# Delta rule, second pair of heads: its first half beside the first pair's chain, and one attention head projected later

## The chip, the cores and the metric

The kernel runs on one core of a Trainium2 chip. The metric is the device time of one execution in microseconds (us). A core has five engines that run side by side, each with its own queue of instructions: TensorE (PE in the profile; its weight loads are PEld), VectorE (DVE), ScalarE (ACT), GpSimd (POOL) and SyncE (SP). SP, ACT and POOL can issue transfers (DMA). An instruction waits for the results it needs and for the buffer it writes, and everything behind it on its engine waits with it.

## The reference

A decoder trunk with two layers, 512 tokens and width 1024. The change lies in the mixer of the first ("even") layer: four heads of the gated delta rule (A) and four heads of differential attention (B).

```python
qkv_a, z_a, b_a, a_a, q_b, k_b, v_b = split_cols(h @ w_in, EVEN_SPLITS)
...
kk = jnp.einsum('bhncd,bhnsd->bhncs', kb, k) * decay
a_mat = jnp.where(strict, kk, 0.0) + jnp.eye(C, dtype=kk.dtype)
...
sol = lax.linalg.triangular_solve(a_mat, rhs, left_side=True, lower=True, unit_diagonal=True)
u, w = sol[..., :dv], sol[..., dv:]
...
k_dec = k * jnp.exp(gc[..., -1:] - gc)[..., None]
...
def step(S, xs):
    qd, kd, uc, wc, qkc, gl = xs
    v_new = uc - jnp.einsum('bhcd,bhde->bhce', wc, S)
    o = jnp.einsum('bhcd,bhde->bhce', qd, S) + jnp.einsum('bhcs,bhse->bhce', qkc, v_new)
    S = S * gl[..., None, None] + jnp.einsum('bhcd,bhce->bhde', kd, v_new)
    return S, o
```

Each B head makes two softmax maps of 512 x 512 (causal), takes their difference, multiplies by its values and normalises. The eight heads' outputs go through one output projection. Behind the mixer come an MLP and a gated embedding, then the second layer, which the change does not touch.

## The kernel before

The even mixer takes about the first 313 us of the span. Projections run as matmuls of 128 x 128 weights against 512 tokens in f32r, each factor split into a high and a low part (`whl`, `act`), into three PSUM accumulators (`mm`); smaller work of the A heads uses two further PSUM buffers (`aux()`, written `ax` in the profile), that of the B heads three (`aux2()`, also `ax`).

All heads are Python generators, and `even_mixer` ends in a loop that writes the program: a chain (a head's generator) is resumed when the TensorE time counted so far has reached the due time that its last `yield` set; while none is due, the next step of a projection is written. So a `yield 10.0` asks for a certain amount of other TensorE work before the chain's next instruction. The projections come in the order of the table `ORDER`: a0 to a3 make the queries and keys of the A heads, w0 and w2 the values of a pair, v0 and v1 the values of B, b0 to b3 queries and keys of a B head. What is written in this order is what each engine then executes in order.

`gdn_head(h, qT, kT)` is one A head. Its first half makes the decay (`b`, `et`, from `decays`), the product of keys (`pg`), the keys by token (`pk`), their squared norms (`kk`), the decayed keys `kd`, the matrix `u` to be inverted, its small 16 x 16 diagonal blocks (`ag`, for a pair of heads in `lc`), their scales (`pb`, in the profile `ax<-xc,gmask`), the scores of queries and keys (`ax<-qT,kT`) and the scaled values `vb`. Then it waits until the small blocks of its pair are inverted (`pair in solved`). The second half builds the whole inverse from the small ones: `x` and its transpose `z`, level by level (`ax<-x,ub`, `ax<-z,yy`), then the chain of four states, and the normed output, which is called `u` again (its transposes are `ax<-gen,u`).

`small_inverses(pair)` is spawned by the second head of a pair behind its `pb`. It writes the blocks `lc` to DRAM (`lsc`), reads them back with a row spread over sixteen partitions (`lb`, eight transfers on ScalarE's queue), yields 10, runs fifteen steps of two GpSimd operations each (`xt`, `xc`), yields 10 and marks the pair as solved.

`ABREAST = 2` heads run at a time: heads 2 and 3 start only when head 0, or 1, is done, and when the values of their pair are there.

`diff_head` is a B head: scores of two maps in blocks of 128 rows (`ax<-hl`, `ax<-kl,hl`), softmax on VectorE and ScalarE, transposed probabilities (`ax<-gen,p`), the product with the values (`ax<-hl,at`), and at its end `diff_norm` (`dsq`, `dss`, `rs_t`, `do`) with four transposes `ax<-gen,do`. The tiles `hl` are a ring of eight buffers of 4 KB a partition, used for high and low parts (`hl32()` gives one as f32).

Of the kernel before, what the change touches and what calls it, by code (L numbers as in the profile page):

```python
# [10 lines left out]
F32 = mybir.dt.float32  # L11
F32R = mybir.dt.float32r
I32 = mybir.dt.int32
AF = mybir.ActivationFunctionType
ALU = mybir.AluOpType
# [3 lines left out]
P = 128  # L19
T = 512  # L20
NT = T // P
# [3 lines left out]
HA = 4  # L25
# [11 lines left out]
BASE = 16  # L37
# [31 lines left out]
LAT_A, LAT_B = 1.55, 1.7  # L69
W_G, W_B, W_T, W_V, W_Q = 10.0, 22.5, 20.0, 6.0, 3.6  # L70
Z_B, DSTEP = 3, 3.47
ORDER = "a0 a1 w0 v0 v1 b0 b1 a2 a3 w2 b2 b3"
ABREAST = 2
N_SP = 10
N_ST = 5
SRAW, SWHL, SA = 8, 3, 4
ORDER_MID, ORDER_END = (1, 5, 6, 7, 3, 4, 2), (1, 2, 5, 6, 3, 7, 4)
# [20 lines left out]
def trunk(ctx: ExitStack, tc: tile.TileContext, I, cst, out):  # L98
    nc = tc.nc
    V, S, G, PE = nc.vector, nc.scalar, nc.gpsimd, Tensor(tc)  # L100
# [13 lines left out]
    def aux():  # L114
        return pax.tile([P, T], F32, tag="ax", name="ax", bufs=2)
# [8 lines left out]
    def hl32():  # L124

        return hlp.tile([P, 2, T], F32, tag="hl", name="hl32")
# [12 lines left out]
    def v3(ap):  # L139
        return ap.rearrange("p (i c) -> p i c", c=P)  # L140
# [23 lines left out]
    ident, m_le, m_gt = (gen[:, j * P:(j + 1) * P] for j in range(3))  # L164
# [157 lines left out]
    def even_mixer(act, first, wba):  # L322
        w_in = I["w_in_even"][0]
        with ExitStack() as es:
            gp = es.enter_context(tc.tile_pool(name="gp", bufs=1))
            def sp(name):
                return gp.tile([P, T], F32, tag="sp", name=name, bufs=N_SP)

            def st_(name):
                return gp.tile([P, T], F32, tag="st", name=name, bufs=N_ST)  # L330
# [81 lines left out]
            def hcol(name, h):  # L412
                return st[name][:, :, h]

            def bc(ap):
                return ap.broadcast_to([P, NT, P])
# [16 lines left out]
            def small_inverses(pair):  # L433

                lc, n = small_l[pair], 2 * NT
                lsc = dp.tile([P // BASE, BASE * n * BASE], F32, tag="lsc", name="lsc", bufs=1)
                nc.scalar.dma_start(lsc.rearrange("b (r n) -> b r n", r=BASE), lc.rearrange("p h i c -> p (h i c)"))
                lb = gp.tile([P, BASE, n, BASE], F32, tag="lb", name="lb", bufs=1)
                for a in range(P // BASE):
                    nc.scalar.dma_start(lb[a * BASE:(a + 1) * BASE].rearrange("p r i c -> p (r i c)"),  # L440
                                        lsc[a:a + 1, :].broadcast_to([BASE, BASE * n * BASE]))
                yield 10.0
                xc = small_w[pair].rearrange("p h i c -> p (h i) c")
                tmp = gp.tile([P, n, BASE], F32, tag="xt", name="xt", bufs=1)
                for c in range(BASE - 1, 0, -1):
                    G.tensor_tensor(out=tmp[:, :, 0:c], in0=lb[:, c, :, 0:c],
                                      in1=xc[:, :, c].broadcast_to([P, n, c]), op=ALU.mult)
                    G.tensor_tensor(out=xc[:, :, 0:c], in0=xc[:, :, 0:c], in1=tmp[:, :, 0:c], op=ALU.add)
                yield 10.0
                solved.append(pair)  # L450

            def gdn_head(h, qT, kT):
                while len(done) < h + 1 - ABREAST or h >= ABREAST and h not in vts:
                    yield 2.0
                if h >= ABREAST:
                    yield from decays(h)
                blk = [slice(i * P, (i + 1) * P) for i in range(NT)]

                pair, sub = h // 2, h % 2
# [3 lines left out]
                pk = aux()  # L463
                for i in range(NT):
                    PE.transpose(pk[:, blk[i]], kT[:, blk[i]], ident)
                sq, kk = st_("sqk"), gp.tile([P, 2, NT], F32, tag="kk", name="kk", bufs=ABREAST)
                for i in range(NT):
                    S.activation(out=sq[:, blk[i]], in_=pk[:, blk[i]], func=AF.Square, accum_out=kk[:, 0, i:i + 1])
                kd = sp("kd")
                S.activation(out=kd, in_=pk, func=AF.Copy)  # L470
                dg = st_("dg")
                V.tensor_tensor(out=v3(dg), in0=v3(pg), in1=mid(gm["minus_base"]), op=ALU.mult)
                second = pair in small_l
# [5 lines left out]
                while h not in decay or "ec" not in st:  # L479
# [13 lines left out]
                                in1=s.broadcast_to([P, NT, BASE]), op=ALU.mult)  # L493
# [9 lines left out]
                                op=ALU.mult)  # L503
# [4 lines left out]
                for i in range(NT):  # L508
                    PE.matmul(pq[:, blk[i]], lhsT=kT[:, blk[i]], rhs=qT[:, blk[i]], start=True, stop=True)
                V.tensor_tensor(out=et, in0=pq, in1=et, op=ALU.mult)  # L510
                G.tensor_tensor(out=v3(kd), in0=v3(kd), in1=bc(hcol("ekd", h)), op=ALU.mult)

                pq = aux()
                for i in range(NT):
# [1 line left out]
                sq, eq = st_("sqq"), kk[:, 1]  # L516
# [11 lines left out]
                V.tensor_tensor(out=v3(vb), in0=v3(pv), in1=bc(n2), op=ALU.mult)  # L528
                yield 2.0

                while pair not in solved:
                    yield 1.0
                x, xc = sp("x"), small_w[pair][:, sub]
                for i in range(NT):
                    G.tensor_tensor(out=x[:, blk[i]].rearrange("p (b c) -> p b c", c=BASE),
                                    in0=xc[:, i, :].unsqueeze(1).broadcast_to([P, P // BASE, BASE]),
                                    in1=gm["minus_base"].rearrange("p (b c) -> p b c", c=BASE), op=ALU.mult)
# [13 lines left out]
                for lv in LEVELS:  # L551
                    y, wide, full = st_("yy"), lv < 32, lv == P // 2
                    ub = u
                    if not full:
# [5 lines left out]
                        else:  # L560
                            for j in range(64 // lv):
                                c = slice((2 * j + 1) * lv, (2 * j + 2) * lv)
                                G.tensor_tensor(out=cut(ub, lv)[:, j::64 // lv], in0=v3(u)[:, :, c],
                                                in1=mu[:, c].unsqueeze(1).broadcast_to([P, NT, lv]), op=ALU.mult)
# [11 lines left out]
                    else:  # L576
                        for j in range(64 // lv):
                            S.activation(out=y[(2 * j + 1) * lv:(2 * j + 2) * lv, 0:T // 2],
                                         in_=py[j * lv:j * lv + lv, 0:T // 2], func=AF.Copy)
# [8 lines left out]
                    else:  # L588
                        for j in range(64 // lv):
                            zo = half(z[2 * j * lv:(2 * j + 1) * lv], lv, 1)[:, j::64 // lv]  # L590
                            V.tensor_tensor(out=zo, in0=zo, in1=cut(pt[j * lv:j * lv + lv], lv)[:, j::64 // lv],
                                            op=ALU.subtract)
# [908 lines left out]
```

## Time and profile before

| | us |
|---|---|
| median of 3 runs (1420.2 to 1420.65) | 1420.47 |
| the profiled execution's own time | 1421.96 |
| its span, first to last instruction | 1420.2 |
| TensorE busy | 1384.1 |
| VectorE busy | 867.3 |
| ScalarE busy | 773.5 |
| GpSimd busy | 174.2 |

The mean granted clock of TensorE over the span is 0.989 of full speed. Times in the rows count from the span's start. A time in brackets behind a row is how long the engine stood idle before that instruction, and behind the arrow what it waited for. An f32 matmul leaves two records in the profile, so one `pb` counts twice there.

### The profile page before, as it was taken

To read this page: it belongs to the slowest core of one execution; us is meant where nothing else is said; L and a number is where in the kernel's file an instruction comes from. 1 tells how busy PE (TensorE), PEld (TensorE's weight loads), DVE (VectorE), ACT (ScalarE), POOL (GpSimd) and SP (SyncE) were. 2 spreads that over 40 slices of the span, in tenths; PEclk is the share of its full clock that TensorE was granted. 3 is DMA by queue.
4 is the path that set the end of the run, shared out by engine and by line. 5 is a ranking of instruction groups with operands and counts; after the bars stand their busy time and mean duration, and the time that the engine had idled before them with its cause. 6 is when DMAs were issued, how large, how long until landed. Compare 5 with 4: busy or idle time off the path is not lost. (4 is left out here: it accounts for less than half of the span.)

```text
span 1420.2 us, 18495 instructions
## 1 busy us (share of the span) xinstructions
PE 1384.1 (97%) x6969; PEld 1152.2 (81%) x6969; DVE 867.3 (61%) x1535; ACT 773.5 (54%) x1304; POOL 174.2 (12%) x231
## 2 busy tenths in 40 slices
PE   8999987999999999999999999999999999999997
PEld 6887775777888888888878888888888888888887
DVE  6837786665465665657665746646646565655865
ACT  6746775663555564556534545535355555554643
POOL 1350056010110201101001000000011020101100
PEclk9999998999999999999999999999999999999999
DMA  6251213114954856566333443852295476756611
GB/s 179 79 106 46 60 31 77 45 55 168 250 135 136 176 154 160 140 159 129 93 72 60 60 89 60 79 97 90 89 270 135 132 153 174 159 143 146 132 60 60
DMA packets 134238, 164.61 MB, mean 116 GB/s; under 512 B 9650, under 2 KB 91396, under 8 KB 133892
## 3 DMA queue, kind: packets, MB, share of 16 engines
q1 hardware_dynamic: 113968, 123.82, 32.6%
q0 software_dynamic: 15360, 33.56, 13.8%
q10 hardware_dynamic: 4820, 6.05, 1.9%
q8 instruction: 55, 0.90, 0.3%
q14 instruction: 35, 0.29, 0.1%
HBM read 152.78 MB, written 2.23 MB: 109 GB/s over the span
## 5 line engine op out<-in xcount | busy, mean ns | idle before, releaser
L90 PE MATMUL mm<-act,whl 128*128 128x512 f32 (+1 forms) x2784 | 657.9, 389 | 2.6 <-DVE whl L149 1.9
L90 PEld LDWEIGHTS mm<-act,whl 128*128 128x128 f32 x2784 | 506.3, 190 | 103.0 <-DVE whl L149 3.2
L90 PE MATMUL ax<-swhl,sa 128*128 128x512 f32 x1344 | 314.0, 389 | 0.0
L90 PEld LDWEIGHTS ax<-swhl,sa 128*128 128x128 f32 x1344 | 252.1, 188 | 52.4
L149 DVE TENSOR_TENSOR whl<-raw,whl 128x1024 fp32r<-128x1024 f32 x139 | 170.6, 1228 | 167.5 <-ACT whl L146 164.7
L149 DVE TENSOR_TENSOR swhl<-sraw,swhl 128x1024 fp32r<-128x1024 f32 x112 | 136.9, 1222 | 124.4 <-ACT swhl L146 124.2
L146 ACT ACTIVATE whl<-raw 128x1024 fp32r<-128x1024 f32 (+1 forms) x140 | 147.9, 1057 | 54.5 <-PE mm L90 50.2
L146 ACT ACTIVATE swhl<-sraw 128x1024 fp32r<-128x1024 f32 x112 | 118.8, 1060 | 101.2 <-PE ax L90 86.7
L90 PE MATMUL mm<-whl,act 128*128 128x256 f32 (+2 forms) x720 | 108.0, 307 | 0.2 <-ACT act L146 0.2
L1261 ACT ACTIVATE r<-mm 128x512 f32<-128x512 f32 x64 | 38.2, 597 | 126.0 <-PE mm L90 125.9
L90 PEld LDWEIGHTS mm<-whl,act 128*128 128x128 f32 x720 | 97.0, 190 | 6.7 <-ACT act L146 0.7
L1165 POOL DMA_DIRECT2D sraw<-w_mlp_down x48 | 57.5, 1218 | 251.0 <-DVE swhl L149 115.6
L319 DVE TENSOR_TENSOR x_tok<-x_tok,ax 128x512 f32<-128x512 f32 x114 | 73.5, 681 | 10.8 <-PE ax L90 10.7
L90 PE MATMUL mm<-owhl,act 128*128 128x256 f32 (+1 forms) x336 | 57.9, 329 | 0.0
L90 PE MATMUL mm<-owhl,hl 128*128 128x512 f32 x228 | 54.8, 397 | 0.0
L90 PEld LDWEIGHTS mm<-owhl,act 128*128 128x128 f32 x336 | 49.6, 188 | 6.4
L312 POOL TENSOR_TENSOR rn<-tn,nhalf 128x1 f32<-128x1 f32 x12 | 6.6, 553 | 385.9 <-DVE tn L311 385.9
L1165 POOL DMA_DIRECT2D sraw<-sraw x16 | 14.6, 915 | 302.5 <-DVE swhl L149 276.2
L90 PEld LDWEIGHTS mm<-owhl,hl 128*128 128x128 f32 x228 | 42.4, 188 | 10.1
L1174 ACT ACTIVATE sraw<-sraw 128x1024 f32<-128x1024 f32 x32 | 33.8, 1058 | 27.0 <-DVE swhl L149 17.5
L146 ACT ACTIVATE act<-ax 128x512 fp32r<-128x512 f32 x40 | 22.4, 595 | 43.1 <-PE ax L94 42.9
L149 DVE TENSOR_TENSOR sa<-hl,sa 128x512 fp32r<-128x512 f32 x64 | 43.8, 685 | 0.0
(341 smaller groups left out, 1609.6 us busy)
## 6 DMA issues: line engine op xcount, KB each, us to landing
raw<-w_mlp_up SPq DMA_DIRECT2D x64, 512.0 KB, 4.3
sraw<-w_mlp_down SPq DMA_DIRECT2D x64, 512.0 KB, 3.9
sraw<-w_mlp_down POOLq DMA_DIRECT2D x48, 512.0 KB, 5.8
raw<-w_in_even SPq DMA_DIRECT2D x32, 256.0 KB, 3.5
sraw<-sraw POOLq DMA_DIRECT2D x16, 512.0 KB, 6.3
raw<-w_ple_gate SPq DMA_DIRECT2D x16, 512.0 KB, 4.9
raw<-w_in_odd SPq DMA_DIRECT2D x16, 512.0 KB, 5.2
raw<-w_in_odd SPq DMA_DIRECT2D x32, 256.0 KB, 6.6
```

The source lines that it names most:

```text
L90: return self.tc.nc.tensor.matmul(out, lhsT=lhsT, rhs=rhs, start=start, stop=stop, skip_group_check=onto)
L146: S.activation(out=hi, in_=src, func=AF.Copy)
L149: return (E or V).tensor_tensor(out=lo, in0=src, in1=hi.bitcast(F32), op=ALU.subtract)
L312: G.tensor_tensor(out=r, in0=t, in1=nhalf[:, 0:1], op=ALU.pow)
L319: V.tensor_tensor(out=x_tok[i][:, cs], in0=x_tok[i][:, cs], in1=ps, op=op)
L1165: G.dma_start(o, t, accum_op=ALU.add)
L1174: S.activation(out=t, in_=t, func=AF.Copy, scale=-1.0)
L1261: S.activation(out=r, in_=ps, func=AF.Relu)
```

## The change

Heads 2 and 3 no longer wait at their start for heads 0 and 1. They wait only for their values, do their first half, and wait for `done` where they already wait for the small inverses. Since `kd` of heads 2 and 3 would have to be kept over that time, it is not made in the first half: the keys are transposed again behind the wait, and VectorE makes `kd` from them. The ring `sp` grows from 10 to 14 tiles and `kk` from two to four; the 8 KB buffer `lb` is replaced by two tiles of the ring `hl`, filled by sixteen transfers of 64 KB in place of eight of 128 KB. In `ORDER`, b1 moves behind w2.

```diff
-ORDER = "a0 a1 w0 v0 v1 b0 b1 a2 a3 w2 b2 b3"
+ORDER = "a0 a1 w0 v0 v1 b0 a2 a3 w2 b1 b2 b3"
-N_SP = 10
+N_SP = 14
...
-                lb = gp.tile([P, BASE, n, BASE], F32, tag="lb", name="lb", bufs=1)
+                lbs = [hl32().rearrange("p a (r i c) -> p (a r) i c", r=BASE // 4, c=BASE) for _ in range(2)]
+                part = BASE // 2 * n * BASE
                 for a in range(P // BASE):
-                    nc.scalar.dma_start(lb[a * BASE:(a + 1) * BASE].rearrange("p r i c -> p (r i c)"),
-                                        lsc[a:a + 1, :].broadcast_to([BASE, BASE * n * BASE]))
+                    for j, lb in enumerate(lbs):
+                        nc.scalar.dma_start(lb[a * BASE:(a + 1) * BASE].rearrange("p r i c -> p (r i c)"),
+                                            lsc[a:a + 1, j * part:(j + 1) * part].broadcast_to([BASE, part]))
                 yield 10.0
...
-                    G.tensor_tensor(out=tmp[:, :, 0:c], in0=lb[:, c, :, 0:c],
+                    G.tensor_tensor(out=tmp[:, :, 0:c], in0=lbs[c // 8][:, c % 8, :, 0:c],
...
-                while len(done) < h + 1 - ABREAST or h >= ABREAST and h not in vts:
+                while h >= ABREAST and h not in vts:
                     yield 2.0
...
-                kd = sp("kd")
-                S.activation(out=kd, in_=pk, func=AF.Copy)
+                if h < ABREAST:
+                    kd = sp("kd")
+                    S.activation(out=kd, in_=pk, func=AF.Copy)
...
-                G.tensor_tensor(out=v3(kd), in0=v3(kd), in1=bc(hcol("ekd", h)), op=ALU.mult)
+                if h < ABREAST:
+                    G.tensor_tensor(out=v3(kd), in0=v3(kd), in1=bc(hcol("ekd", h)), op=ALU.mult)
...
-                while pair not in solved:
+                while pair not in solved or len(done) < h + 1 - ABREAST:
                     yield 1.0
+                if h >= ABREAST:
+                    kd, pk = sp("kd"), aux()
+                    for i in range(NT):
+                        PE.transpose(pk[:, blk[i]], kT[:, blk[i]], ident)
+                    V.tensor_tensor(out=v3(kd), in0=v3(pk), in1=bc(hcol("ekd", h)), op=ALU.mult)
```

What this does to the order of TensorE's work is shown at three places.

The first is the end of head 0 and head 1. Before, the outputs `u` of heads 0 and 1 are transposed first, and the first matmuls of head 2 (`ax<-b,m_gtr`) come behind them:

```order
L90 MATMUL ax<-state,qT 128x128
L90 MATMUL mm<-act,whl 128x512 x9
L94 MATMUL ax_1954<-gen,p_1737 128x128 x3
L90 MATMUL mm<-act,whl 128x512 x6
L94 MATMUL ax<-gen,u 128x128 x4
L90 MATMUL mm<-act,whl 128x512 x7
L94 MATMUL ax<-gen,u 128x128 x4
L90 MATMUL ax<-b,m_gtr 128x512 x2
```

Now the same transposes (`ax<-gen,u`) stand behind the `pb` of head 3 (`ax<-xc,gmask`, its first half's last step but the queries and the values):

```order
L90 MATMUL ax<-xc,gmask 128x64
L90 MATMUL ax<-qT,kT 128x128 x4
L90 MATMUL mm<-act,whl 128x512 x2
L94 MATMUL ax<-gen,qT 128x128 x4
L90 MATMUL mm<-act,whl 128x512
L94 MATMUL ax<-gen,u 128x128 x4
L90 MATMUL mm<-act,whl 128x512 x4
L94 MATMUL ax<-gen,vT 128x128 x8
L94 MATMUL ax_2029<-gen,do 128x128 x4
L90 MATMUL mm<-act,whl 128x512
L94 MATMUL ax<-gen,u 128x128 x4
L90 MATMUL mm<-act,whl 128x512 x32
```

Heads 2 and 3 have moved ahead by most of their first half, and the second pair's small inverse now runs beside the end of heads 0 and 1.

The second is the stretch between that `pb` and the first transposes of `x`. Before, it begins with the scores of queries and keys and a long run of projections, then come the scores of a B head:

```order
L90 MATMUL ax<-qT,kT 128x128 x4
L94 MATMUL ax<-gen,qT 128x128 x4
L90 MATMUL mm<-act,whl 128x512 x5
L94 MATMUL ax<-gen,vT 128x128 x8
L90 MATMUL mm<-act,whl 128x512 x47
L90 MATMUL ax_2305<-hl 128x256
L90 MATMUL ax_2305<-kl,hl 128x256
L90 MATMUL ax_2316<-hl 128x256
L90 MATMUL ax_2316<-kl,hl 128x256
L94 MATMUL ax_2330<-gen,do 128x128 x4
L90 MATMUL mm<-act,whl 128x512 x9
L90 MATMUL ax_2338<-hl 128x256
```

Now the run of projections is the one of 32 above, and this is the end of the stretch, with `x` as its last row:

```order
L90 MATMUL mm<-act,whl 128x512 x8
L90 MATMUL ax_2057<-hl 128x256
L90 MATMUL ax_2057<-kl,hl 128x256
L90 MATMUL ax_2068<-hl 128x256
L90 MATMUL ax_2068<-kl,hl 128x256
L90 MATMUL ax_2091<-hl 128x256
L90 MATMUL ax_2091<-kl,hl 128x256
L90 MATMUL mm<-act,whl 128x512 x3
L90 MATMUL ax_2102<-hl 128x256
L90 MATMUL ax_2102<-kl,hl 128x256
L90 MATMUL mm<-act,whl 128x512 x3
L94 MATMUL ax<-gen,x 128x128 x4
```

The long run has become shorter, by the work of heads 0 and 1 and by eight new transposes of the keys (`ax<-gen,kT`) that stand between the two pieces shown.

The third is the end of the mixer, before the output projection's last part (`whl,hl`). Before, the last delta heads' `u` and the last B head's `do` come in this way:

```order
L90 MATMUL ax<-vn,et 128x128
L90 MATMUL ax<-state,qT 128x128
L90 MATMUL mm<-whl,hl 128x512 x5
L94 MATMUL ax<-gen,u 128x128 x4
L90 MATMUL mm<-whl,hl 128x512 x7
L94 MATMUL ax<-gen,u 128x128 x4
L90 MATMUL mm<-whl,hl 128x512 x6
L94 MATMUL ax_3165<-gen,do 128x128 x4
L90 MATMUL ax_3240<-whl,hl 128x512 x6
```

Now the last B head is the last to finish, its blocks (`ax<-hl,at` and `ax<-gen,p`) among the output projection:

```order
L90 MATMUL ax_3159<-hl,at 128x128 x3
L90 MATMUL mm<-whl,hl 128x512 x9
L94 MATMUL ax_3164<-gen,p_3135 128x128 x4
L90 MATMUL mm<-whl,hl 128x512 x4
L90 MATMUL ax_3171<-hl,at 128x128 x4
L90 MATMUL mm<-whl,hl 128x512 x3
L94 MATMUL ax_3191<-gen,do 128x128 x4
L90 MATMUL ax_3266<-whl,hl 128x512 x12
```

The delta heads' `u` have moved away from the end, and the product with the values stands three projections before the transposes of `do`.

## Rows read from the trace of the kernel before

**Rows 1.** The page: the span, and busy time, share and instructions of each engine.

```profile
span 1420.2 us, 18495 instructions
...
PE 1384.1 (97%) x6969; PEld 1152.2 (81%) x6969; DVE 867.3 (61%) x1535; ACT 773.5 (54%) x1304; POOL 174.2 (12%) x231
```

**Rows 2.** Waits of TensorE, 87 to 345: total, how often, longest, in us.

```profile
PE ax L94 <- POOL x L535: 7.1, 2, 6.8
PE ax L94 <- DVE u L649: 3.3, 3, 2.1
```

**Rows 3.** Windows of 20 us: busy by engine (PE first), clock, DMA share, GB/s.

```profile
180.00:200.00 20.00, 17.89 (x93) 14.90 (x92) 17.50 (x32) 15.80 (x39) 10.38 (x9) 0.91 0.19 53
240.00:260.00 20.00, 18.16 (x78) 14.52 (x78) 9.93 (x27) 10.65 (x25) 6.72 (x13) 0.61 0.01 2
300.00:320.00 20.00, 17.78 (x89) 13.77 (x88) 12.90 (x25) 11.39 (x26) 3.03 (x3) 1.00 0.28 81
```

**Rows 4.** Timeline of TensorE, second pair: start, us, instruction, [idle before].

```profile
210.20 0.43 PE L90 MATMUL ax<-xc,gmask 128*128 128x64 f32 x2 [0.26 <-DVE et L510]
...
213.14 0.66 PE L94 MATMUL ax<-gen,qT 128*128 128x128 f32 x4 [1.55 <-DVE lc L502]
...
214.94 1.09 PE L94 MATMUL ax<-gen,vT 128*128 128x128 f32 x8
215.79 10.96 PE L90 MATMUL mm<-act,whl 128*128 128x512 f32 x47
...
241.45 0.48 PE L94 MATMUL ax<-gen,x 128*128 128x128 f32 x1 [6.75 <-POOL x L535]
```

**Rows 5.** Timeline of ScalarE and its queue, second pair.

```profile
213.11 0.34 ACTq L437 DMA_DIRECT2D lsc<-lc  x1
...
215.97 4.97 ACTq L440 DMA_DIRECT2D lb<-lsc  x5
220.98 1.19 ACT L702 ACTIVATE rot<-mm 32x512 f32<-32x512 f32 x2 [4.69 <-DMA raw<-w_in_even]
```

**Rows 6.** Timeline of GpSimd, second pair.

```profile
225.73 0.54 POOL L446 TENSOR_TENSOR xt<-lb,xc 128x120 f32<-128x120 f32 x1 [2.18 <-DMA lb<-lsc]
...
229.21 0.36 POOL L446 TENSOR_TENSOR xt<-lb,xc 128x96 f32<-128x96 f32 x1
229.65 1.25 POOL L448 TENSOR_TENSOR xc<-xc,xt 128x96 f32<-128x96 f32 x1
...
240.95 3.83 POOL L535 TENSOR_TENSOR x<-xc,gmask 128x128 f32<-128x128 f32 x8
```

**Rows 7.** Timeline of ScalarE and its queue, first pair.

```profile
70.20 0.34 ACTq L437 DMA_DIRECT2D lsc<-lc  x1
...
72.62 2.79 ACTq L440 DMA_DIRECT2D lb<-lsc  x6
75.45 0.38 ACT L662 ACTIVATE hl<-mm 128x256 f32<-128x256 f32 x1 [2.92 <-PE mm L90]
```

**Rows 8.** Tile lb: from issue to landing of its sixteen transfers.

```profile
DMA to landing us min/median/max: 3.7/5.7/7.3
```

**Rows 9.** Timeline of GpSimd, first pair.

```profile
81.83 0.40 POOL L446 TENSOR_TENSOR xt<-lb,xc 128x120 f32<-128x120 f32 x1 [7.90 <-DMA lb<-lsc]
...
95.70 3.41 POOL L535 TENSOR_TENSOR x<-xc,gmask 128x128 f32<-128x128 f32 x8
```

**Rows 10.** Timeline of VectorE, end of the mixer.

```profile
308.08 0.68 DVE L939 TENSOR_REDUCE dss<-dsq 128x4 f32<-128x512 f32 x1
```

**Rows 11.** Timeline of TensorE, end of the mixer.

```profile
307.48 0.63 PE L94 MATMUL ax<-gen,u 128*128 128x128 f32 x4 [0.90 <-DVE u L649]
...
310.03 0.66 PE L94 MATMUL ax<-gen,u 128*128 128x128 f32 x4 [0.30 <-DVE u L649]
...
313.09 0.63 PE L94 MATMUL ax<-gen,do 128*128 128x128 f32 x4 [1.02 <-DVE do L942]
```

**Rows 12.** Timeline of TensorE, a level of the first pair.

```profile
130.57 1.46 PE L90 MATMUL ax<-z,yy 128*64 128x64 f32 x16 [0.72 <-ACT yy L578]
```

More of the change, by code (lines that the diff above doesn't have):

```diff
@@ L465, in gdn_head @@
                     PE.transpose(pk[:, blk[i]], kT[:, blk[i]], ident)
-                sq, kk = st_("sqk"), gp.tile([P, 2, NT], F32, tag="kk", name="kk", bufs=ABREAST)
+                sq, kk = st_("sqk"), gp.tile([P, 2, NT], F32, tag="kk", name="kk", bufs=HA)
                 for i in range(NT):
                     S.activation(out=sq[:, blk[i]], in_=pk[:, blk[i]], func=AF.Square, accum_out=kk[:, 0, i:i + 1])
-                kd = sp("kd")
-                S.activation(out=kd, in_=pk, func=AF.Copy)
+                if h < ABREAST:
+                    kd = sp("kd")
+                    S.activation(out=kd, in_=pk, func=AF.Copy)
                 dg = st_("dg")
```

## The prediction

> **What bounds the kernel now.** I read the page's engine totals first [rows 1]: TensorE is busy for 97% of the span, so the time can only change through work that TensorE gains or loses, stretches in which it waits, and its clock. Then came what TensorE waits for in the stretch that the diff touches [rows 2], the second half of the first layer's mixer. The longest entry is the second delta pair's small inverse: TensorE stands 7.1 us for `x`, which GpSimd makes. Behind it stands `u` with 3.3 us in three waits, one of them 2.1. Of the shorter ones the change can reach `lc` with 1.55 us, `do` with 1.02 and `yy` with 0.72 [rows 4, 11, 12]. The third view is the windows of 20 us [rows 3], for the granted clock after those waits: 0.91 where TensorE had waited 2.1 us for `u`, 0.61 behind the wait for `x`, 1.00 around the short waits at the end of the mixer. A window of 20 us at 0.61 has lost 20 x 0.39 = 7.8 us, one at 0.91 has lost 1.8 us. So the inverse costs 7.1 us of waiting and about as much again in clock, the wait for `u` costs 2.1 and 1.8.
>
> Last I followed the inverse through its engines. The second head's matmul `pb` (written `ax<-xc,gmask`) starts at 210.20 [rows 4]. ScalarE's queue sends `lc` to DRAM at 213.11 and issues eight broadcasts back, the last five in a row of 4.97 us, in which ScalarE computes nothing (4.69 us idle) [rows 5]. GpSimd starts its thirty small operations at 225.73 and `x` at 240.95 [rows 6]; TensorE gets `x` at 241.45. From `pb` to `x` that is 31.25 us. TensorE has 24.5 us until it stands (241.45 - 6.75 - 210.20), of which 1.55 are the wait for `lc`, so 22.95 us of work cover the chain.
>
> **The change part by part.** *The earlier first half.* The order shows that heads 2 and 3 now have `pb` behind them before head 0's `u` is transposed; before, they began behind it. Between head 1's last state product and its `u` 22 projections stood, and TensorE waited 2.1 us; now 34 stand there, 7.9 us at 0.233 each (below), and the small matmuls of heads 2 and 3. So the wait goes, with the 1.8 us of clock: -3.9 us (bounds -3.9 and 0). It could stay only if VectorE, which makes `u`, fell behind by the several us that this adds.
>
> *The cover of the small inverse.* An earlier chain helps only if more TensorE work lies between `pb` and `x`. It does not: both ends moved forward together, since the two yields of 10 in `small_inverses`, by which the loop places `x`, are as they were. Counted in the order, from the second head's `pb` to the first transpose of `x`: before, 72 projections of 512 columns, 16 transposes, four `qT,kT` matmuls and eight scores; now 58 projections, 32 transposes (eight of them the new ones of `kT`), and the same matmuls and scores. The run of 47 projections gives 10.96 / 47 = 0.233 us for one, the eight transposes of `vT` take 0.85 us to the next start, 0.106 each [rows 4]. So the cover changes by -14 x 0.233 + 16 x 0.106 = -1.6 us, to 21.4 us.
>
> *The chain itself.* It now brings the same bytes in 16 issues of half the size. Eight more issues at the spacing of the first pair's (six in 2.79 us, 0.47 each [rows 7]) hold ScalarE 3.7 us longer; at the spacing of the second pair's last five (4.97 / 5, about 1.0 each) 8 us longer. How much of this reaches GpSimd is not in the trace: a broadcast lands 3.7 to 7.3 us after its issue [rows 8], and half a transfer may land sooner. From `lsc` to `x` the first pair took 25.5 us (70.20 to 95.70 [rows 7, 9]), the second 27.84. So the bounds for the chain are -2.3 us (the second pair as quick as the first) and +8 us. I take +2, nearer to the first pair's spacing with part of it hidden in the landing. The wait for `x` is then 31.25 + 2 - 21.4 - 1.55 = 10.3 us against 7.1: +3.2 us, with bounds -1.1 and +9.2. The low clock behind it stays, since the wait does; I put its change at 0 (-1 to +3).
>
> A rule speaks against this edit. The rows say only that eight 128 KB transfers cost ScalarE 5 us of idle and GpSimd a start 4.8 us after the last issue ended (220.94 to 225.73) [rows 5, 6]. The Trainium skill, page "DMA: Bandwidth & Descriptors", section "Rules for kernel authors", says that many small transfers should become one large one, and that splitting a transfer into partition halves gains nothing because both halves share the same 16 engines. By it the sixteen transfers carry sixteen fixed costs and no more bandwidth, so the chain can't shorten through the split; the sum above would keep its upper half only.
>
> GpSimd's operations also show a second price: among neighbours of about 0.4 us one took 1.25 us [rows 6]. The Trainium skill, page "SBUF — State Buffer", section "Who interferes with whom", says that VectorE and GpSimd take a shared port by an exclusive lock, the loser standing for the whole instruction. The two `kd` products that leave GpSimd and the two that VectorE gains lie outside the thirty operations or in front of `x`; I count them at nothing.
>
> *kd made again.* Eight more transposes are 0.85 us of TensorE, none hidden, since it is the bound; the new order also cuts its work into more pieces (936 rows against 921). I take +1.0 us (0.85 to 1.6). ScalarE loses two copies and GpSimd two products, all idle cover; VectorE gains two products from PSUM, which lie in front of the wait for `x` and are hidden by it. If that cover went, they would cost at most their own length.
>
> *The end of the mixer.* Head b1 now stands behind w2, so b2 and b3 come later too, and b3's blocks lie among the output projection. Before, the last wait for `do` is 1.02 us and the two for `u` 0.90 and 0.30: 2.2 us in all, with the clock at 1.00. In the order after, the last `hl,at` matmuls of b3 have three projections (0.7 us) between them and the transposes of `do`. The chain from the reduction of `dsq` to that transpose took 308.08 to 313.09, 5.0 us [rows 10, 11]. So a wait of about 5.0 - 0.7 = 4.3 us stands there; those for `u` go, with more projections ahead of them. Waiting: +2.1 us (0 to +4). For clock a wait of 4.3 us lies between the one of 2.1 (1.8 us lost) and the one of 6.75 (7.8 lost): I take +2.5 us, bounds 0 and 7.8.
>
> *The first pair.* Its broadcasts are split too, and ScalarE must evacuate `hl<-mm` at 75.45, right behind the last issue [rows 7]; 3.7 us more there may leave TensorE without a free accumulator. Its `x` is ready at about 96 and not used until 115, so the chain itself has slack. Later the new order leaves two score matmuls (0.7 us) between `ax<-x,ub` and `ax<-z,yy` of a level, where 1.9 us of work stood and TensorE still waited 0.72 us for `yy` [rows 12]: +1.2 us. Together I take +1.3 (0 to +4).
>
> *Sharing the banks.* The first half of heads 2 and 3 and the chain of heads 0 and 1 now take turns in two `ax` buffers. The trace has no such stretch; the nearest waits are `lc`, 1.55 us, and `u`, 0.90. I take +0.9, bounds -1.5 (the wait for `lc` goes) and +4.
>
> **Sum.** +1.0 - 3.9 + 3.2 + 2.1 + 2.5 + 1.3 + 0.9 = +7.1 us. On the profiled execution's own 1421.96 us that is about 1429; the median of the runs shown is 1.5 us lower, so the forecast is 1427 us. The bounds of the terms don't fall together; the case's own range is 1421 to 1435.
>
> **The rivals.** *The wait for `x` is covered.* If the chain takes what the first pair's took and the small waits of the crowded stretch fall inside it, TensorE arrives late enough: 7.1 us of waiting shrink to about 2, and with them 5 of the 7.8 us of clock. With -3.9 for `u` and the +7.8 of the other terms this gives -6, 1414 us. For it: the first pair's 25.5 us. Against it: 21.4 us of cover is still under even that chain, which with `pb` to `lsc` and the hand-over needs 28.9.
>
> *The effects cancel.* The split costs nothing, the end of the mixer keeps its clock: -3.9 for `u`, +1.2 for `x` (8.3 us instead of 7.1, the chain as long as before), +2.1 for the end and +1 to +2 for the rest: about +1, and 1421 us. For it: waits as short as those at 300 to 320 left the clock at 1.00 [rows 3].
>
> *ScalarE's queue becomes the bound.* Sixteen issues at 1.0 us hold it 8 us longer in both pairs; the first pair's projections then stand for accumulators about 4 us, and `x` of the second comes 9 us later than its cover: 1436 to 1440 us. It decides from about 0.8 us an issue, the price between 0.47 and 1.0. Against it: the first pair's spacing.
>
> *The change does less than it says.* If the scheduler kept heads 2 and 3 behind heads 0 and 1, only the split, the transposes and the order of b1 would count; the order shows that it did not, so I give it no chance of its own.
>
> **How the numbers follow.** Forecast 0.53, covered 0.22, cancelled 0.15, queue-bound 0.10. The range is 1414 to 1437: the covered case's centre to the queue-bound case's edge. What a measurement can tell from no change is 0.2%, 2.8 us, so the same is 1417.6 to 1423.3. Slower: the queue-bound case and nearly all of the forecast's, 0.10 + 0.50 = 0.60. The same: most of the cancelled case and a part of the forecast's and the covered one's, 0.17. Faster: the rest, 0.23.
>
> **What would show it.** In the profile after: no wait for `u` before the second inverse; a wait of TensorE for `x` of 8 to 12 us with a window at about 0.6 behind it; sixteen broadcasts on ScalarE's queue with more than 6 us of idle behind them; a last wait for `do` of about 4 us. The forecast is wrong if the wait for `x` is under 5 us, or if the clock behind it stays near 1.

## The result and the profile after

The changed kernel takes 1428.03 us (median of 4, 1426.85 to 1430.9) against 1420.34 before on the same chip. The ratio is 1.0057, with the interval [1.004, 1.0075]: slower by 0.57%. The forecast was 1427. The profiled execution is the slowest of the four (its own time 1430.9, 8.9 us over the one of before), so the account below explains 8.9 us, of which a typical run has 7.7.

The page after has the same shape as [rows 1]; TensorE has gained 2.9 us of busy time, the span 8.9:

```profile
span 1429.1 us, 18544 instructions
...
PE 1387.0 (97%) x6977; PEld 1152.0 (81%) x6977; DVE 862.2 (60%) x1537; ACT 765.0 (54%) x1297; POOL 172.0 (12%) x229
```

What TensorE waits for, after, from 60 to 350 us (columns as in [rows 2]):

```profile
PE ax L94 <- DVE do L951: 7.4, 3, 4.7
PE ax L94 <- POOL x L544: 7.1, 1, 7.1
PE mm L90 <- ACT hl L671: 2.5, 1, 2.5
PE ax L94 <- DVE spare L315: 1.9, 1, 1.9
...
PE ax L94 <- DVE u L658: 0.2, 1, 0.2
```

The waits of this stretch sum to 24.0 us; before they were 18.7. The wait for `u` of 2.1 us is gone. The wait for `x` is as long as it was, `do` has grown from 1.0 to 7.4 (4.7 of it at the end of the mixer), and `hl`, the first pair's accumulators, is new. The windows of 20 us, where the clock is not 1.00 (columns as in [rows 3]):

```profile
80.00:100.00 20.00, 19.64 (x120) 18.04 (x120) 4.92 (x4) 8.66 (x14) 15.56 (x38) 0.91 0.41 107
180.00:200.00 20.00, 16.79 (x87) 13.12 (x86) 14.25 (x30) 7.98 (x25) 8.86 (x9) 0.91 0.34 89
200.00:220.00 20.00, 12.55 (x49) 8.52 (x48) 9.73 (x26) 11.40 (x21) 12.23 (x30) 0.77 0.07 20
220.00:240.00 20.00, 18.07 (x95) 13.28 (x96) 10.93 (x33) 10.09 (x27) 6.27 (x13) 0.81 0.09 26
320.00:340.00 20.00, 20.00 (x83) 16.22 (x82) 10.95 (x12) 10.24 (x16) 0.00 (x0) 0.92 0.76 257
340.00:360.00 20.00, 18.07 (x80) 14.61 (x79) 12.01 (x24) 5.07 (x11) 1.66 (x3) 0.91 0.27 85
```

Each share below 1 times 20 us: 1.8 + 1.8 + 4.6 + 3.8 + 1.6 + 1.8 = 15.4 us. The same sum before is 13.8 (0.83, 0.91, 0.96 and 0.61 in four windows). But a low clock costs time only while TensorE works, and these sums count it while TensorE stands too. Windows of 5 us around the wait for `x` show the difference, first after, then before:

```profile
210.00:215.00 5.00, 3.76 (x8) 2.00 (x8) 0.03 (x1) 1.44 (x4) 4.25 (x11) 0.56 0.00 0
215.00:220.00 5.00, 0.00 (x0) 0.00 (x0) 4.60 (x15) 3.79 (x8) 4.21 (x12) 0.50 0.00 0
220.00:225.00 5.00, 4.03 (x14) 3.19 (x15) 1.24 (x5) 0.25 (x2) 4.84 (x11) 0.50 0.00 0
225.00:230.00 5.00, 5.00 (x20) 3.53 (x19) 1.36 (x4) 2.56 (x7) 0.06 (x1) 0.73 0.00 0
```

```profile
240.00:245.00 5.00, 3.17 (x13) 2.47 (x14) 2.91 (x7) 1.48 (x5) 4.84 (x11) 0.50 0.02 5
245.00:250.00 5.00, 5.00 (x15) 3.27 (x15) 2.69 (x8) 4.06 (x8) 1.00 (x1) 0.50 0.01 2
250.00:255.00 5.00, 5.00 (x19) 4.31 (x18) 1.71 (x5) 2.37 (x6) 0.87 (x2) 0.50 0.00 0
255.00:260.00 5.00, 5.00 (x36) 4.47 (x35) 2.61 (x8) 2.74 (x8) 0.00 (x0) 0.95 0.00 0
```

The clock is at half, the lower of its two levels (1.2 of 2.4 GHz), for about 17 us in both kernels. After, it falls before the wait for `x`, and TensorE stands through 7.1 us of the slow time. Busy time by missing share gives 5.0 us after (1.65 + 0 + 2.0 + 1.35) and 6.8 before. Summed in this way in steps of 0.5 us, from 60 to 380 us, the clock costs 11.4 us after and 11.7 before. So it explains none of the loss. By the page, idle time grew by 6.0 us (span minus TensorE's busy time: 42.1 against 36.1), 5.3 of them the waits of this stretch, and busy time by the 2.9 us.

The second pair's inverse, which was to become cheaper by starting earlier, is read from three engines. TensorE after, from the second head's `pb` to the transposes of `x`:

```profile
185.64 0.41 PE L90 MATMUL ax<-xc,gmask 128*128 128x64 f32 x2 [0.31 <-DVE rs_t L250]
...
192.38 0.66 PE L94 MATMUL ax<-gen,do 128*128 128x128 f32 x4 [1.85 <-DVE do L951]
...
194.13 1.11 PE L94 MATMUL ax<-gen,u 128*128 128x128 f32 x4 [0.86 <-DVE vT L532]
...
210.09 1.46 PE L90 MATMUL mm<-act,whl 128*128 128x512 f32 x3 [1.29 <-DVE a L714]
...
220.97 1.34 PE L94 MATMUL ax<-gen,x 128*128 128x128 f32 x3 [7.13 <-POOL x L544]
```

From `pb` to `x` it is 35.33 us, not 31.25. TensorE keeps going until 213.84, but 4.0 of those 28.2 us are new short waits (1.85 for `do`, 0.86 for `vT`, 1.29 for `a`), and the mean clock of the stretch is 0.88. ScalarE's queue shows where the chain got its length:

```profile
190.15 13.46 ACTq L442 DMA_DIRECT2D hl<-lsc  x16
203.66 0.69 ACT L663 ACTIVATE qT<-ax,cols 128x512 f32<-128x512 f32 x1 [13.85 <-DMA hl<-lsc]
```

Sixteen issues held it for 13.46 us, where the last five of eight had held it for 4.97 [rows 5]. Two narrower views of the same queue, 194 to 196 and 200 to 202, show that the hold is not evenly spread:

```profile
193.80 0.90 ACTq L442 DMA_DIRECT2D hl<-lsc  x2
```

```profile
199.94 2.26 ACTq L442 DMA_DIRECT2D hl<-lsc  x3
```

The tenth transfer was issued by 194.70. The eleventh starts at 199.94. In between lies a weight load of SyncE's queue. The tile `raw`, 180 to 210:

```profile
L182 SPq DMA_DIRECT2D raw<-w_in_even x2: 368/368/368, 186.8 to 196.1; - x2
...
DMA to landing us min/median/max: 3.8/3.8/3.8
```

Its last load is issued at 196.1 and lands 3.8 us later, at 199.94, the moment at which the eleventh transfer starts. The program names the reason. The transfers of both queues take turns on eight completion counters (`DMAHW0` to `DMAHW7`), and the weight load took `DMAHW4` between the third broadcast and the fourth. The eleventh, the next one due for that counter, waits for it. The tenth's row in the program and its own:

```
hl_1956<-lsc 16x1024 [waits DMAHW3_49]
hl_1955<-lsc 16x1024 [waits DMAHW4_49]
```

The weight load itself could only start when VectorE had read the buffer's old contents (making `whl`, which ended at 196.0). So GpSimd's start hangs on a load that has nothing to do with it:

```profile
205.65 0.63 POOL L448 TENSOR_TENSOR xt<-hl,xc 128x120 f32<-128x120 f32 x1 [12.08 <-DMA hl<-lsc]
...
220.47 3.38 POOL L544 TENSOR_TENSOR x<-xc,gmask 128x128 f32<-128x128 f32 x8
```

The kernel before had met the same hold, only shorter. Its eighth broadcast was issued late too (ScalarE's queue, 218 to 222):

```profile
220.63 0.31 ACTq L440 DMA_DIRECT2D lb<-lsc  x1
```

The seventh was out by 217.8, and the eighth starts when a weight load of SyncE's queue, issued at 214.36, has landed 6.2 us later. So 2.8 of the 4.97 us of the last five were this hold. In both pairs and both kernels one issue follows another after 0.47 us where nothing holds it.

The end of the mixer, on TensorE:

```profile
319.69 1.02 PE L94 MATMUL ax<-gen,do 128*128 128x128 f32 x4 [4.70 <-DVE do L951]
```

### The profile page after: what moved, and what is told of

Read it like the earlier page. It is cut to its first block, busy times and chain, and to the rows that moved or that the text cites. A ratio compares the mean times of both kernels' runs of the same rounds, so it can differ in the third digit from the quotient of the medians.

```text
span 1429.1 us, 18544 instructions
## 1 busy us (share of the span) xinstructions
PE 1387.0 (97%) x6977; PEld 1152.0 (81%) x6977; DVE 862.2 (60%) x1537; ACT 765.0 (54%) x1297; POOL 172.0 (12%) x229
## 4 chain that ended last, share of the span: by engine, by line
PE 83%; DVE 4%; ACT 4%; POOL 3%; DMA 2%; issue 2%; ACTq 1%; SPq 0%; POOLq 0%; DVEq 0%
PE mm L90 51%; PE ax L90 29%; PE ax L94 3%; DMA raw<-w_ple_gate 1%; POOL xc L450 1%; POOL xt L448 1%; ACTq L442 1%; DMA sraw<-w_mlp_down 1%; DVE whl L149 1%; ACT whl L146 0%; DVE owhl L149 0%; DMA hl<-lsc 0%; DMA raw<-w_mlp_up 0%; ACT rot L711 0%; POOL rot L715 0%
## 5 line engine op out<-in xcount | busy, mean ns | idle before, releaser
L90 PEld LDWEIGHTS mm<-whl,act 128*128 128x128 f32 x720 | 98.5, 193 | 10.3 <-ACT hl L671 2.7
```

Of the source, the lines that this page charges most:

```text
L90: return self.tc.nc.tensor.matmul(out, lhsT=lhsT, rhs=rhs, start=start, stop=stop, skip_group_check=onto)
```

## The experiments

Ratios are to the kernel before on the same chip; its median was 1421.5 to 1422.1 us in these runs, so the changed kernel's 1.0057 stands for about 1430 there.

**The split alone.** The kernel before with sixteen transfers into the ring `hl`.

```diff
-                lb = gp.tile([P, BASE, n, BASE], F32, tag="lb", name="lb", bufs=1)
+                lbs = [hl32().rearrange("p a (r i c) -> p (a r) i c", r=BASE // 4, c=BASE) for _ in range(2)]
...
+                    for j, lb in enumerate(lbs):
...
```

> The kernel before with one part of the change: the small blocks come in sixteen transfers of 64 KB into two tiles of the ring hl. Theory A (the split holds ScalarE's queue, and this is what the change lost): ScalarE stands 6 to 7 us behind the first pair's issues, TensorE waits 2 to 3 us for hl there and loses about 2 us of clock, the second pair's x comes 3 to 5 us later: 1428 us (1425 to 1431). Theory B (the loss comes from the place of b1, at the end of the mixer): not over 1422 us.

1425.65 us, ratio 1.0032 [1.0019, 1.0044]. Its waits, 60 to 380 us, and its queue:

```profile
PE ax L94 <- POOL x L537: 8.7, 1, 8.7
...
PE mm L90 <- ACT hl L664: 2.5, 1, 2.5
```

```profile
221.90 2.60 ACT L146 ACTIVATE hl<-a 64x512 fp32r<-64x512 f32 x4 [7.64 <-DMA hl<-lsc]
```

The wait for `hl` of 2.5 us is there, TensorE waits 1.6 us more for `x` than before, ScalarE stands 7.6 us behind the second pair's issues. Theory B, by which the split costs nothing and the loss lies in b1's place, falls; the size is in A's range, at its low end.

**The order alone.** The kernel before with b1 behind w2.

```diff
-ORDER = "a0 a1 w0 v0 v1 b0 b1 a2 a3 w2 b2 b3"
+ORDER = "a0 a1 w0 v0 v1 b0 a2 a3 w2 b1 b2 b3"
```

> The kernel before with the new ORDER alone (b1 behind w2). Theory A: the wait of about 4.5 us for do at the end of the mixer appears here too, with 3 us of clock, while the wait for u stays: 1424 us (1421 to 1428), about half of the loss. Theory B: all of the loss, 1427 us or more.

1425.54 us, ratio 1.0029 [1.0015, 1.0044]. A's time came out, but not by A's way:

```profile
PE ax L90 <- ACT qT L654: 4.4, 1, 4.4
...
PE ax L94 <- DVE do L942: 2.0, 1, 2.0
```

`do` costs 2.0 us and not 4.5; the most goes to a wait of 4.4 for `qT` in the middle of the mixer. The two losses added make 1.0061, the change 1.0057. If they add, the earlier first half, with the keys transposed again, brought about nothing. No run shows that they do, and by the intervals the first half could be worth some 4 us either way.

**The moved wait without the order.** The changed kernel with the old ORDER, and eight transfers of two source rows.

```diff
-                for a in range(P // BASE):
+                for a in range(0, P // BASE, 2):
...
-                                            lsc[a:a + 1, j * part:(j + 1) * part].broadcast_to([BASE, part]))
+                                            lsc[a:a + 2, j * part:(j + 1) * part].unsqueeze(1).broadcast_to([2, BASE, part]))
```

> The changed kernel with the old ORDER and eight transfers: left of the change are the moved wait, the kd made again and the larger rings. In the order of instructions heads 2 and 3 then still start behind head 0's u, since their values come last. Theory A: only the eight transposes count: 1421 us (1420 to 1423), the wait for x about 7 us. Theory C (the second kd and the shared banks cost more than their transposes): 1424 us or more.

1449.27 us, ratio 1.0192 [1.0178, 1.0206]. It doesn't answer the question, since the transfers turned out slow, as the next run shows. The order of its instructions does tell one thing: heads 2 and 3 start behind head 0's `u`, as before, since their values are projected last. So the moved wait alone does not bring their start forward; it needs the moved b1.

**Eight transfers in the changed kernel.** The same edit of the transfers, with the new ORDER.

> The changed kernel with eight transfers of 128 KB (32 partitions each) in place of sixteen of 64 KB, into the same two tiles. Theory A: the wait for hl of 2.5 us goes with its 1.8 us of clock, x comes 4 us sooner, its wait falls from 7.1 to about 3 us and the clock behind it gives 3 us back: 1417 us (1414 to 1421). Theory B: the end of the mixer and the shared banks are untouched, so 1426 to 1428 us.

1450.72 us, ratio 1.0206 [1.0191, 1.0222], over 20 us above either theory. GpSimd's start in the first pair, and the DMA engines in two windows (last two columns: busy share, GB/s):

```profile
98.59 0.40 POOL L448 TENSOR_TENSOR xt<-hl,xc 128x120 f32<-128x120 f32 x1 [24.58 <-DMA raw<-w_in_even]
```

```profile
72.00:76.00 4.00, 4.00 (x37) 4.00 (x36) 1.69 (x4) 0.61 (x6) 2.01 (x3) 1.00 0.09 29
76.00:80.00 4.00, 1.60 (x14) 1.37 (x13) 0.00 (x0) 0.78 (x3) 0.00 (x0) 1.00 0.12 47
```

From the first issue at 71.84 to GpSimd's start are 26.7 us (10.1 before: 71.77 to 81.83, [rows 9]), and the DMA engines are busy for a tenth of the time. (The row names `raw`, a weight load that landed at about that moment; GpSimd reads only the broadcasts, whose last one landed at 98.5.) A transfer of two source rows to 32 partitions keeps few of them busy. One row to 16 partitions had kept them all, as the kernel before shows:

```profile
75.00:77.00 2.00, 2.00 (x20) 2.00 (x18) 0.18 (x1) 1.33 (x2) 0.00 (x0) 1.00 1.06 131
```

So the run tells nothing about the number of issues. The Trainium skill, page "DMA: Bandwidth & Descriptors", section "Rules for kernel authors", says that an outermost dimension under 16 confines a transfer to at most as many engines. Two of sixteen are 0.125; the rows with 0.09 and 0.12 agree. The expectation counted issues alone and left the spread over the engines out.

**Two transfers, and one.** If the spread goes with the source rows, eight rows in one transfer should keep half of the engines busy. The changed kernel with two transfers, and the kernel before with one:

```diff
+                for j in (1, 0):
+                    nc.scalar.dma_start(lbs[j].rearrange("p r i c -> p (r i c)"),
+                                        lsc[:, j * part:(j + 1) * part].unsqueeze(1).broadcast_to([P // BASE, BASE, part]))
```

> The changed kernel with two transfers of 512 KB (all 128 partitions, the half needed first ahead) in place of sixteen. Eight transfers of two source rows each moved only about 53 GB/s at a tenth of the DMA engines; if the spread goes with the number of source rows, eight rows move about 210 GB/s and the 1 MB lands in 5 to 6 us. Theory A (ScalarE's queue, held by the issues and by a weight load that the eleventh waits for, makes x late): x comes 6 to 8 us sooner, TensorE's wait for x goes from 7.1 to under 1.5, the wait for hl goes, the clock stays up: 1411 us (1406 to 1417). Theory D (the rate per transfer is what counts, and a single transfer is as slow as in the eight): x later than now by over 15 us, 1445 us or more.

> The kernel before with one transfer of 1 MB in place of eight of 128 KB, into lb. Theory A: the chain from lsc to x falls from 27.8 to about 23 us, the wait for x from 6.75 to 2 to 3 us and half of the clock behind it comes back: 1413 us (1409 to 1418). Theory D: 1440 us or more.

With two, the changed kernel takes 1418.64 us, ratio 0.9981 [0.9972, 0.999]: 0.76% less than with sixteen, though short of A's 1406 to 1417. So sixteen transfers in place of two cost more than the whole loss. The edit changes the number of issues, sends the half that is needed first ahead and meets other completion counters, and no run takes these apart. Much of the gain is clock: from 60 to 380 us, over the time TensorE works, it costs 3.8 us here and 11.4 with sixteen. With one, the kernel before takes 1420.96, ratio 0.9998 [0.999, 1.0007]: no gain, where A had 1413. Two transfers, second pair, on GpSimd, VectorE and TensorE:

```profile
192.28 0.55 POOL L447 TENSOR_TENSOR xt<-hl,xc 128x120 f32<-128x120 f32 x1 [2.89 <-DMA hl<-lsc]
...
204.57 1.26 POOL L714 TENSOR_TENSOR rot<-rot,sinr 128x512 f32<-128x512 f32 x1
```

```profile
205.87 0.92 DVE L715 TENSOR_TENSOR a<-a,rot 128x512 f32<-128x512 f32 x1 [7.98 <-POOL rot L714]
```

```profile
210.74 0.66 PE L94 MATMUL ax<-gen,x 128*128 128x128 f32 x2 [7.53 <-DVE kd L540]
```

The DMA engines' share in the first pair is 0.51, half of them, as eight rows let expect:

```profile
75.00:77.00 2.00, 2.00 (x19) 2.00 (x19) 0.36 (x1) 1.73 (x3) 0.00 (x0) 1.00 0.51 115
```

GpSimd starts 10.8 us after `pb` (181.46), where it needed 20.0. But TensorE still waits 7.5 us, for another reason: the product of `rot` for b1 stands behind the thirty operations on GpSimd, VectorE waits 8.0 us for it, and `kd`, made at 209.92 from the accumulator that the transposes of `x` need, stands behind that on VectorE. In the kernel before with one transfer, VectorE waits in the same way; there the transfer is also no quicker (12.4 us from issue at 72.02 to GpSimd's start):

```profile
84.40 0.40 POOL L445 TENSOR_TENSOR xt<-lb,xc 128x120 f32<-128x120 f32 x1 [10.19 <-DMA lb<-lsc]
```

```profile
237.71 0.72 DVE L706 TENSOR_TENSOR a<-a,rot 128x512 f32<-128x512 f32 x1 [9.07 <-POOL rot L705]
```

**The end of the mixer.** The changed kernel, and the one with two transfers, with the projection's pairs in another order.

```diff
-w, pairs = I["w_out_even"][0], (0, 2, 3, 1)
+w, pairs = I["w_out_even"][0], (0, 2, 1, 3)
```

> The changed kernel with the output projection's pairs of heads in the order 0, 2, 1, 3 (the delta heads 2 and 3 before the attention heads b2 and b3), so that twelve projections instead of three stand between b3's last product and the transposes of do. Theory A: the wait for do falls from 4.7 to about 2.6 us and the clock behind it stays up: 1424 us (1421 to 1427). Theory E (what waits there is given back at the owhl weights or at spare): no change, 1428 us.

> The changed kernel with both: two transfers and the pairs in the order 0, 2, 1, 3. Theory A: the gains add, 1407 us (1402 to 1414). If they share a wait, no better than the two transfers alone.

1426.63 us, ratio 1.0042 [1.0028, 1.0055], and 1418.04, ratio 0.9977 [0.9968, 0.9987]. The first kernel's waits:

```profile
PE ax L94 <- DVE do L951: 5.2, 3, 2.5
PE ax L94 <- DVE spare L315: 3.6, 1, 3.6
```

The last wait for `do` is 2.5 us instead of 4.7, as expected; `spare`, some 27 us later, waits 3.6 instead of 1.9. Against the kernels without this edit (1.0057 and 0.9981) the intervals overlap, so no gain is shown, and the 1407 expected of the two edits together did not come. Theory E, that the wait is given back further on, agrees with `spare`.

**`rot` on VectorE.** Three kernels: the changed one with two transfers, the changed one with its sixteen, and the kernel before with one.

```diff
-G.tensor_tensor(out=rot, in0=rot, in1=sinr, op=ALU.mult)
+V.tensor_tensor(out=rot, in0=rot, in1=sinr, op=ALU.mult)
```

> The changed kernel with two transfers and the product of rot with the sines on VectorE instead of GpSimd. In the run with two transfers x was ready 11 us sooner after pb, and TensorE waited 7.5 us for a kd that stood behind VectorE's 8.0 us wait for rot, the rot product being queued behind GpSimd's thirty operations. Theory A (GpSimd's thirty operations still hold the second pair, now by way of rot): without rot in that queue TensorE waits 1 to 3 us in front of x and the clock stays up: 1411 us (1407 to 1415). Theory F (VectorE's eight further operations of 0.7 us cost as much as they free): 1418 us or more.

> The changed kernel with rot's product on VectorE alone, the sixteen transfers kept. Theory A: x is still as late, its wait stays at 7 us and the wait for hl at 2.5 us: 1427 us (1425 to 1429). Theory G (rot alone holds the changed kernel): 1420 us or less.

> The kernel before with one transfer of 1 MB and rot's product on VectorE. Its one transfer took about 12 us to land, so GpSimd starts no sooner than in the kernel before. Theory A: the wait of 8.1 us behind rot becomes a wait for x of 5 us: 1418 us (1415 to 1421). If the earlier first half of the change is worth nothing once both paths are free, this kernel is as quick as the changed one with the same two edits; theory A says 5 us or more slower.

The first takes 1424.67 us, ratio 1.0013 [0.9999, 1.0026]: not 1411, and slower than with `rot` on GpSimd. TensorE's wait in front of `x` fell from 7.5 to 4.9 us, the sum of its waits stayed at 20 us (1.6 for `xc` and others are new), and the clock fell twice. F's time came out, 1418 us or more; the profile puts it on the clock. Windows of 5 us:

```profile
210.00:215.00 5.00, 5.00 (x15) 3.54 (x14) 0.82 (x3) 1.01 (x4) 1.63 (x4) 0.50 0.00 0
215.00:220.00 5.00, 4.31 (x20) 2.92 (x19) 3.52 (x9) 2.42 (x6) 0.00 (x0) 0.99 0.00 0
220.00:225.00 5.00, 4.40 (x15) 2.94 (x14) 2.96 (x10) 3.06 (x7) 0.00 (x0) 0.69 0.00 0
...
235.00:240.00 5.00, 5.00 (x37) 4.15 (x35) 2.07 (x12) 3.17 (x10) 0.00 (x0) 0.60 0.01 3
```

After the wait for `x` the clock is back by 215, but it falls again at about 222 and stays low until 238, where TensorE had waited only 0.7 and 0.6 us (0.69 at 219.8, 0.60 at 222.2). In the kernel with two transfers alone it stayed at 1.00 from 215 on. Of the twelve runs of this kernel three took 1418.2 to 1418.7 us, with mean clocks of 0.993 to 0.995, the others 1423.0 to 1426.5, with 0.986 to 0.991.

With sixteen transfers, `rot` on VectorE makes it worse: 1434.51 us, ratio 1.0089 [1.0074, 1.0104], expected 1427. Theory G falls, and A's size too: the wait for `x` stays (7.5 us), and TensorE waits longer elsewhere (1.6 for `xc`, which is new, and 1.7 for `a`, where it was 1.3).

The kernel before with one transfer and this edit is the quickest: 1416.19 us, ratio 0.9964 [0.9952, 0.9976], quicker than both kernels of this study. Its waits:

```profile
PE ax L94 <- POOL x L534: 6.0, 1, 6.0
PE ax L94 <- DVE u L648: 3.3, 3, 2.1
```

The wait behind `rot` (8.1 us) became one for `x` of 6.0, as expected, and `u` still waits its 2.1.

The expectation also set this kernel against the changed one with two transfers and `rot` on VectorE, and had it 5 us or more slower. It is 8.5 us quicker (1416.19 against 1424.67 on the same chip), and the three quickest runs of the other, at 1418.2 to 1418.7, lie above its median. So with `rot` out of GpSimd's queue the change's order shows no gain; the number of transfers differs between the two, one against two. With `rot` left on GpSimd it is the other way: 1418.64 with the change and two transfers, 1420.96 without it and one.

**All three.** The changed kernel with two transfers, `rot` on VectorE and the pairs 0, 2, 1, 3.

> The changed kernel with two transfers, rot's product on VectorE, and the output projection's pairs in the order 0, 2, 1, 3. Theory A: 1410 us (1406 to 1415), the pairs giving back about as little as beside the two transfers alone, since the wait for do that goes is found again at spare.

1422.27 us (1414.38 to 1424.38), ratio 0.9998 [0.9984, 1.0013]: no gain, where 1410 was expected. The spread goes with the clock again, 0.996 in the quickest run and 0.989 in the slowest.

## Why the prediction was right

Its time (1427 against 1428.03), its sign and its main reading, that the cover of the small inverse doesn't grow by moving both ends, held. From `pb` to the moment it stands TensorE works 24.2 us at a mean clock of 0.88, about 21 us at the full one; 21.4 had been counted. Of the signs that it named, the vanished wait for `u`, the long idle time behind the sixteen broadcasts and the wait for `do` came. A wait for `x` of 8 to 12 us with a clock of about 0.6 behind it did not: it is 7.1, with 0.77 and 0.81, though not so far off as its two signs of being wrong (under 5 us, or a clock near 1). That the sum came within about a microsecond is luck, since single terms were off by up to 4.5 us and cancelled. Term by term:

- *`u`, -3.9.* The wait went, the gain did not stay. In its place b0's `do` (1.85) and `vT` (0.86) make TensorE wait 2.7 us at the same spot, and the window 180 to 200 has the same 0.91 as before. The prediction counted the projections in front of `u` and not the two other matmuls that now stand there with their own chains. This is its largest miss.
- *`x`, +3.2.* The wait stayed at 7.1. Two errors cancel. The chain grew by 4.1 us, twice the 2.0 taken (inside the bounds). The cover grew as much by the new waits and the lower clock within it, which are themselves lost time. The chain's growth was taken from the spacing of issues, with "about 1.0 each" for the second pair; that figure held 2.8 us of the wait for a weight load ([rows 5] names it, `raw<-w_in_even`). After, the same hold is 5.2 us, more than the whole growth of the chain.
- *The clock behind `x`, 0.* By windows of 20 us it looks right, 8.4 us lost and 8.6 before (0.8 + 7.8). Over the time that TensorE works it is 5.0 against 6.8, a gain of about 2 us. The prediction's way of counting, window by missing share, took in time in which TensorE stood.
- *The end of the mixer, +2.1 and +2.5.* The wait for `do` came out as 4.7 (4.3 forecast) and the clock lost 1.7 behind it. Not in the forecast was `spare`, 27 us later: its wait grew from 0.8 to 1.9, with another 1.7 us of clock. From 300 to 380 us waiting and clock together went from 3.5 to 10.4 us, the largest loss of any stretch. The runs with the pairs turned show no gain here.
- *The first pair, +1.3.* `hl` waits 2.5 us and 1.7 us of clock go with it, three times the term. But the waits for `hl` of a B head and `whl` near 105 us (2.8 and 1.1, with 3.2 us of clock) shrank to 0.5, so that waiting and clock from 60 to 120 us fell from 7.1 to 5.0 us. They fell as far with the split alone (5.1), and hardly with the order alone (7.0).
- *The transposes and the banks, +1.9.* Work grew by about 3 us, of which the eight transposes were to be 0.85; what the rest is, no run shows. Short waits of 1.5 us came (0.9 for `z` among them), and the waits for `lc` (1.55) and `yy` (0.72) went, the second against the forecast.

The queue-bound rival set ScalarE's queue as the bound, at about 1.0 us an issue. Its hold came in the second pair (13.46 us for sixteen), but not by its price: the issues cost 0.47 each, as in the first pair, and 5.2 us are the wait for a completion counter. The chain grew by 4.1 us, not 8. No case had a load on another queue standing between two issues, though the kernel before already had one. The covered rival is what the kernel with two transfers became, in part: 0.9981, with the wait moved from GpSimd's `x` to VectorE's `kd`.

What stays open: what the earlier first half is worth by itself, and why. With two transfers it waits for `rot`; with `rot` moved the clock falls a second time, and the order before with one transfer is quicker.

## What to carry to other kernels

Before starting a chain earlier, count the work between its two ends: if a planner moves both, the wait at the end stays, and only the link that is slow by itself (here a broadcast through DRAM) shortens it. A transfer's issue is an instruction in a queue: more and smaller ones hold everything behind them, and through a shared completion counter they can wait for a load of another queue. So take the price of an issue from rows in which nothing holds the queue. Count a low clock only over the time in which the engine works. When a wait goes, ask which instruction stands next in that engine's order; three of the gains here (`u`, `x`, `do`) turned up as waits for the next one.

## What was not expected of the hardware

- How many DMA engines a broadcast transfer keeps busy goes with its number of source rows and not with its size: shares of 1.06 and 0.12 for one row and two at the same 128 KB, 0.51 for eight rows. From the first issue to GpSimd's start 1 MB took 10.1 us as eight transfers of one row, 26.7 as eight of two, 12.4 as one of eight; with two of eight rows GpSimd starts on the first half after 6.7 us (72.12 to 78.78).
- Transfers of two queues took turns on the same completion counters, and a broadcast waited 5.2 us for a weight load (2.8 us before).
- The granted clock fell to 0.5 for some 17 us about two waits of 0.7 and 0.6 us, in a stretch that had just come back from a fall. In three runs of twelve the higher mean clock suggests that it did not; only one run of the twelve has a profile. The quick runs and the others lie about 7 us apart, nearly as much as the whole change.
